# A hybrid decoder step on Trainium2: weight additions by feature tile, squares and forms of the last pair one product later, an embedding scaled on ScalarE

## The chip, the cores and the metric

The kernel runs on one core of one Trainium2 chip. The metric is the device time of one execution in microseconds (us); the median of three runs of the kernel before is 1403.98 us (1400.8 to 1405.53). A core has five engines that each take their instructions in order: TensorE (PE in the profile, with its weight loads as PEld), VectorE (DVE), ScalarE (ACT), GpSimd (POOL) and SyncE (SP), which here only issues DMA transfers. An instruction of one engine that needs the result of another waits at the head of its queue, and all that is queued behind it waits too.

## The reference, cut to what matters

One layer of a decoder on 1024 new prompt positions and 8 single new tokens (1032 columns in all): a mixer, a squared-ReLU MLP, and a per-layer input embedding, each added to the residual.

```python
x = x + jnp.concatenate([o, sg.astype(x.dtype)], axis=-1) @ w_out
x = x + jnp.square(jax.nn.relu(rms_norm(x, g_ff) @ w_up)) @ w_down
x = x + (p @ w_ple) * jax.nn.sigmoid(rms_norm(x, g_ple) @ w_ple_gate)
```

Here `w_up` is 1024 x 4096 and `w_down` 4096 x 1024. The change lies in the product with `w_down` and in the preparation of `p` (`p_prompt`, 1024 x 256). All arithmetic is float32.

## The kernel before, in words

Float32 products are made of three matmuls each: a weight block is split into a rounded part `whi` (ScalarE, line 150) and its remainder `wlo` (VectorE, line 153), the other operand into `hi` and `lo`, and whi·hi, wlo·hi and whi·lo are added in PSUM (lines 1473 to 1475). Such a pair `whi`, `wlo` is called a form here; a ring holds four of them.

The down projection (`down`, some 340 us of the span, from 905 to 1244 us) splits its 4096 rows into four groups j, and does each group by seven products in place of eight (P1, P6, P7, P4, P2, P5, P3 in that order, a scheme of Strassen's kind). That makes 28 products, n = 0 to 27, in the list `seq`. Each product has four feature tiles p, each with its own form, two token halves t, and 12 matmuls for each: 96 matmuls. PSUM results go by VectorE into `u2`, `u3` and `acc` (lines 1480 and 1482).

What a product needs:

- Its moving operand. It was computed by the up projection and lies in DRAM (`f_d`). `load_raw` (line 1356) brings it in two halves into the single buffer `raw`, ScalarE casts each half (`hi`, line 1363), VectorE subtracts (`lo`, line 1364). `split_raw(n + 1)` and `load_raw(n + 2)` stand at the start of product n.
- Its forms, taken four ahead from the generator `down_forms`. P1, P4, P2 take blocks of the weight as loaded (`a11`, `a22`, `a12`). P6 takes s2 = A21 + A22 - A11, P5 takes s1 = A21 + A22; GpSimd makes both for each p (lines 1385 and 1386). P7 and P3 take a difference `sd` (GpSimd, line 1392), in a buffer of which there is one only: the difference for tile p + 1 is not begun before `whi` and `wlo` of tile p have been made.

Three other pieces run in this stage. (1) The up projection's last pair of tiles is left over: its Relu and Square (ScalarE, line 1225, four passes over `q`) and its forms, six GpSimd subtractions (lines 1229 to 1231) into `late`, which is the memory of the accumulator C22; `dforms_out` (lines 1236 and 1237) stores both to `f_d`, where the products of the fourth group read them, and only then `x1_old` (line 1401) may load the old residual into C22. They stand in product n = 1, the stores in n = 2, the load in n = 3. (2) `x1_old` loads a quarter of the residual (1,056,768 bytes) into C11 at the start, C21 and C12 at n = 0 and 1. (3) `p_prompt` is loaded at the end of n = 12 into the memory of `q` (line 1526) and is scaled by the factor `mst` of its row: eight GpSimd multiplications of 128x256 (line 1530), written after n = 14 to 17.

The order on PE and SP is the one written in the program. On ScalarE, VectorE and GpSimd a scheduler chooses the order when the kernel is built, among instructions that are ready by its own estimate; `tc.high_priority` raises one, and `tc.issue_after(x)` keeps an instruction behind x.

## Time and profile before

| | |
|---|---|
| Median of the runs (lowest, highest) | 1403.98 us (1400.8, 1405.53) |
| The profiled execution's own time | 1404.94 us |
| Its span, first to last instruction | 1403.2 us |
| Mean granted clock of TensorE | 0.971 |
| Busy share of the span: PE, DVE, POOL, ACT | 94%, 64%, 51%, 46% |

The profile is of one execution. Times inside it count from the span's start; 1.74 us of the execution lie outside the span. A granted clock of 1.00 is TensorE's full speed (2.4 GHz), 0.50 its lower level. TensorE is busy for 94% of the whole; what it is not busy for, and where it runs at the lower level, has to be read from the single stretches.

### The profile page before, as it was taken

The numbers are of one execution on the slowest core, as the hardware profiler recorded it, in microseconds if no ns is written. First come the engines' busy times: TensorE is split into PE (matmuls) and PEld (weight loads), VectorE is DVE, ScalarE is ACT, GpSimd is POOL, SyncE is SP. The second block draws the span as 40 slices with busy tenths as digits, with TensorE's granted clock in tenths as the row PEclk, the third lists the DMA queues.
The fourth block names the chain that finished last, engine by engine and source line by source line (L and its number), as shares of the span: only waits on it lengthen the run. The fifth ranks groups of instructions, "written<-read, shape, count | busy, mean of one in ns | idle before, by whom it ended". The sixth has DMA issues, their size and how long they took to land.

```text
span 1403.2 us, 26599 instructions
## 1 busy us (share of the span) xinstructions
PE 1312.5 (94%) x10189; PEld 1280.5 (91%) x10189; DVE 900.7 (64%) x1836; ACT 645.6 (46%) x1353; POOL 708.8 (51%) x724
## 2 busy tenths in 40 slices
PE   6979978999999799899999999889998999899996
PEld 5879978888999799899999999889998999899996
DVE  7755745456946856555545544567976878797554
ACT  7574645632232415556545445443332333346344
POOL 5300888847515404668856787350516215835241
PEclk9999988999999999999999999999999999999998
DMA  7334534646524831244455564658353533232231
GB/s 237 101 91 107 153 92 137 177 135 174 150 84 146 259 90 46 61 137 130 150 149 169 175 212 155 221 191 283 117 184 113 172 122 121 61 102 78 63 121 61
DMA packets 213419, 194.00 MB, mean 138 GB/s; under 512 B 20952, under 2 KB 183451, under 8 KB 213284
## 3 DMA queue, kind: packets, MB, share of 16 engines
q1 hardware_dynamic: 213292, 192.30, 44.5%
q8 instruction: 80, 1.31, 0.4%
q14 instruction: 47, 0.39, 0.1%
HBM read 131.75 MB, written 60.61 MB: 137 GB/s over the span
## 4 chain that ended last, share of the span: by engine, by line
PE 69%; DVE 9%; POOL 9%; ACT 5%; issue 4%; DMA 3%; SPq 1%; POOLq 0%; ACTq 0%; DVEq 0%
PE A L1184 10%; PE D L1184 7%; PE d L1474 6%; PE d L1475 6%; PE d L1473 6%; PE g L209 5%; PE g L211 5%; PE g L210 5%; PE B L1184 3%; PE C L1184 3%; POOL xinv L644 2%; PE g L1702 2%; POOL it L643 2%; DVE wlo L153 2%; PE g L1704 2%
## 5 line engine op out<-in xcount | busy, mean ns | idle before, releaser
L209 PE MATMUL g<-ra,whi 128*128 128x384 f32 (+3 forms) x800 | 272.6, 341 | 0.7 <-ACT ra L388 0.6
L1474 PE MATMUL d<-h,wlo 128*128 128x260 f32 (+1 forms) x896 | 258.2, 288 | 11.0 <-DVE wlo L153 10.5
L1473 PE MATMUL d<-h,whi 128*128 128x260 f32 (+1 forms) x896 | 257.4, 287 | 7.9 <-ACT whi L150 7.9
L1475 PE MATMUL d<-h,whi 128*128 128x260 f32 (+1 forms) x896 | 257.3, 287 | 0.0
L211 PE MATMUL g<-ra,whi 128*128 128x384 f32 (+3 forms) x800 | 256.4, 321 | 0.8 <-POOL ra L389 0.4
L210 PE MATMUL g<-ra,wlo 128*128 128x384 f32 (+3 forms) x800 | 255.2, 319 | 0.0
L1474 PEld LDWEIGHTS d<-h,wlo 128*128 128x128 f32 x896 | 173.4, 194 | 13.3 <-DVE wlo L153 13.2
L1473 PEld LDWEIGHTS d<-h,whi 128*128 128x128 f32 x896 | 173.3, 193 | 8.9 <-ACT whi L150 8.9
L1475 PEld LDWEIGHTS d<-h,whi 128*128 128x128 f32 x896 | 173.2, 193 | 0.0
L209 PEld LDWEIGHTS g<-ra,whi 128*128 128x128 f32 x800 | 154.3, 193 | 2.9 <-ACT ra L388 1.0
L211 PEld LDWEIGHTS g<-ra,whi 128*128 128x128 f32 x800 | 153.7, 192 | 2.5 <-POOL ra L389 1.6
L210 PEld LDWEIGHTS g<-ra,wlo 128*128 128x128 f32 x800 | 154.7, 193 | 0.7 <-DVE wlo L153 0.3
L153 DVE TENSOR_TENSOR wlo<-s,whi 128x512 fp32r<-128x512 f32 x96 | 73.7, 769 | 80.8 <-ACT whi L150 80.4
L153 DVE TENSOR_TENSOR wlo<-st,whi 128x512 fp32r<-128x512 f32 x94 | 75.2, 801 | 39.9 <-ACT whi L150 39.1
L1184 PE MATMUL A<-fb,whi 128*128 128x260 f32 (+1 forms) x512 | 96.6, 281 | 0.0
L643 POOL TENSOR_TENSOR it<-ainv,xinv 32x31 f32<-32x31 f32 (+15 forms) x124 | 73.6, 594 | 39.6 <-DMA ainv<-inv_d 30.3
L150 ACT CAST whi<-s 128x512 fp32r<-128x512 f32 x96 | 59.3, 618 | 73.4 <-PE D L1184 29.1
L1363 ACT CAST h<-raw 128x1024 fp32r<-128x1024 f32 (+1 forms) x56 | 58.8, 1056 | 67.1 <-DMA raw<-f_d 34.7
L644 POOL TENSOR_TENSOR xinv<-xinv,it 32x31 f32<-32x31 f32 (+15 forms) x124 | 82.3, 664 | 9.6
L1225 ACT ACTIVATE q<-q 128x512 f32<-128x512 f32 (+2 forms) x124 | 77.5, 645 | 19.5 <-DVE q L1207 16.0
L1482 DVE TENSOR_TENSOR acc<-acc,d 128x256 f32<-128x256 f32 x192 | 75.0, 413 | 17.8 <-PE d L1475 16.8
L150 ACT CAST whi<-st 128x512 fp32r<-128x512 f32 x96 | 59.0, 619 | 58.2 <-PE g L211 31.4
(450 smaller groups left out, 3526.0 us busy)
## 6 DMA issues: line engine op xcount, KB each, us to landing
a<-in_w_down SPq DMA_DIRECT2D x16, 1024.0 KB
raw<-f_d SPq DMA_DIRECT2D x28, 520.0 KB
raw<-f_d SPq DMA_DIRECT2D x28, 512.0 KB
st<-in_w_in SPq DMA_DIRECT2D x24, 512.0 KB
ck<-ck_d SPq DMA_DIRECT2D x32, 320.0 KB
ra<-in_w_up SPq DMA_DIRECT2D x32, 256.0 KB
rb<-in_w_up SPq DMA_DIRECT2D x32, 256.0 KB
st<-in_w_ple_gate SPq DMA_DIRECT2D x16, 512.0 KB
```

The lines of the kernel that those rows point to most:

```text
L150: S.copy(dst_hi, src)
L153: lo_eng.tensor_sub(dst_lo, src, f32(dst_hi))
L209: PE.matmul(ps[:, :w], lhsT=whi[k], rhs=xh, start=(k == 0), stop=False)
L210: PE.matmul(ps[:, :w], lhsT=wlo[k], rhs=xh, start=False, stop=False)
L211: PE.matmul(ps[:, :w], lhsT=whi[k], rhs=xl, start=False, stop=(k == nk - 1))
L643: G.tensor_mul(tv, a, x)
L644: G.tensor_sub(X[:, j + 1 :, :w], X[:, j + 1 :, :w], tv)
L1184: PE.matmul(ps, lhsT=a[:, k, :], rhs=x[:, c, k, :], start=(first and k == 0 and j == 0), stop=(k == 3 and j == 2), skip_group_check=True)
L1225: placed["act"] = S.activation(v, v, func).ins
L1473: PE.matmul(ps, lhsT=wh[:, k, :], rhs=xh[:, k, :], start=(k == 0), stop=False)
L1474: PE.matmul(ps, lhsT=wl[:, k, :], rhs=xh[:, k, :], start=False, stop=False)
L1475: PE.matmul(ps, lhsT=wh[:, k, :], rhs=xl[:, k, :], start=False, stop=(k == 3))
```

## The change

There are four edits, all in the down projection.

1. In the first group (j = 0), s1 and s2 are kept in order tile by tile: s1 of tile p may not be issued before s2 of tile p - 1.
2. The squares and forms of the up projection's last pair move from product n = 1 to n = 2, behind the cast of product 2's input and behind the last difference issued so far; their stores move from n = 2 to n = 3, just ahead of the load into C22.
3. `x1_old(C11, 0, 0)` goes to the head of `down()`, ahead of the loads of the first input and of A11, A21 and A22 on SP.
4. The scaling of `p_prompt` becomes a ScalarE activation (Copy with a scale for each row), two of them in each of four products, each behind the cast `placed["cast", n]`.

```diff
                         if name == "P6":
-                            G.tensor_add(s1[:, p], a_of("A21", p), a_of("A22", p))
+                            with tc.issue_after(placed["sum"]) if j == 0 and p else ExitStack():
+                                G.tensor_add(s1[:, p], a_of("A21", p), a_of("A22", p))
                             placed["sum"] = G.tensor_sub(s2[:, p], s1[:, p], a_of("A11", p)).ins
...
-                            G.tensor_sub(f, *((a_of("A21", p), a_of("A11", p)) if name == "P7" else (a_of("A12", p), s2[:, p])))
+                            placed["sd"] = G.tensor_sub(f, *((a_of("A21", p), a_of("A11", p)) if name == "P7" else (a_of("A12", p), s2[:, p]))).ins
...
     def down():
+        x1_old(C11, 0, 0)
         load_raw(0)
         load_a(0, "A11")
         load_a(0, "A21")
         load_a(0, "A22")
-        x1_old(C11, 0, 0)
...
-                if n == 1 and p < 2:
+                if n == 2 and p < 2:
                     _, t, q = last[p]
-                    with tc.issue_after(placed["cast", 1]):
+                    with tc.issue_after(placed["cast", 2]):
                         squared(q)
-                    with tc.issue_after(placed["sum"]):
+                    with tc.issue_after(placed["sd"]):
                         dforms_of(t, q, late[t])
...
-            elif n == 2:
+            elif n == 3:
                 for p, t, q in last:
                     dforms_out(p, t, q, late[t])
-            elif n == 3:
                 x1_old(C22, 1, 1)
...
                     x = pt[:, pcol(nn, n - 14), :]
-                    G.tensor_scalar_mul(x, x, mst[:, nn, n - 14 : n - 13])
+                    with tc.issue_after(placed["cast", n]):
+                        S.activation(x, x, AF.Copy, scale=mst[:, nn, n - 14 : n - 13])
```

What this does to the queues is seen at three places. GpSimd first, in the first two products; `sd_11295` is the first difference of P7 (product 2), `s1_11090` and `s2_11091` the sums of the first group, `acc_11038` written from `q8_6118` the forms of the up projection's last pair. Before:

```order
L1392 TENSOR_TENSOR sd_11295<-a21_11069,a11_11072 128x512
L1385 TENSOR_TENSOR s1_11090<-a21_11069,a22_11068 128x512 x4
L1386 TENSOR_TENSOR s2_11091<-s1_11090,a11_11072 128x512 x4
L1229 TENSOR_TENSOR acc_11038<-q8_6118 128x2x256
L1230 TENSOR_TENSOR acc_11038<-q8_6118,acc_11038 128x256
```

After:

```order
L1386 TENSOR_TENSOR s1_11090<-a21_11069,a22_11068 128x512
L1387 TENSOR_TENSOR s2_11091<-s1_11090,a11_11072 128x512
L1386 TENSOR_TENSOR s1_11090<-a21_11069,a22_11068 128x512
L1387 TENSOR_TENSOR s2_11091<-s1_11090,a11_11072 128x512
L1386 TENSOR_TENSOR s1_11090<-a21_11069,a22_11068 128x512
L1387 TENSOR_TENSOR s2_11091<-s1_11090,a11_11072 128x512
L1386 TENSOR_TENSOR s1_11090<-a21_11069,a22_11068 128x512
L1387 TENSOR_TENSOR s2_11091<-s1_11090,a11_11072 128x512
L1393 TENSOR_TENSOR sd_11329<-a21_11069,a11_11072 128x512
L1393 TENSOR_TENSOR sd_11363<-a21_11069,a11_11072 128x512
L1393 TENSOR_TENSOR sd_11397<-a21_11069,a11_11072 128x512
L1229 TENSOR_TENSOR acc_11038<-q8_6118 128x2x256
```

The sums alternate, so that the second tile of s2 is the fourth operation and no longer the sixth, and the first one the second and no longer the fifth; the last pair's forms stand behind the remaining three differences of product 2.

VectorE in the same stretch; `h11_11066` is the remainder `lo` of product 1's input, `wlo_11147` and the names after it the remainders of s2's forms for product 1, `d_...` the PSUM results of product 0. Before:

```order
L1364 TENSOR_TENSOR h11_11066<-raw_11073,h10_11065 128x1024
L1480 COPY u2_11053<-d_11222 128x256
L1482 TENSOR_TENSOR acc_11038<-acc_11038,d_11222 128x256
L1364 TENSOR_TENSOR h11_11066<-raw_11073,h10_11065 128x1040
L1480 COPY u2_11053<-d_11237 128x260
L1482 TENSOR_TENSOR acc_11038<-acc_11038,d_11237 128x260
L153 TENSOR_TENSOR wlo_11147<-s2_11091,whi_11146 128x512
L153 TENSOR_TENSOR wlo_11183<-s2_11091,whi_11182 128x512
L153 TENSOR_TENSOR wlo_11219<-s2_11091,whi_11218 128x512
```

After:

```order
L1364 TENSOR_TENSOR h11_11066<-raw_11073,h10_11065 128x1024
L1481 COPY u2_11053<-d_11165 128x260
L1483 TENSOR_TENSOR acc_11038<-acc_11038,d_11165 128x260
L153 TENSOR_TENSOR wlo_11147<-s2_11091,whi_11146 128x512
L1481 COPY u2_11053<-d_11186 128x256
L1483 TENSOR_TENSOR acc_11038<-acc_11038,d_11186 128x256
L1364 TENSOR_TENSOR h11_11066<-raw_11073,h10_11065 128x1040
L1481 COPY u2_11053<-d_11201 128x260
L1483 TENSOR_TENSOR acc_11038<-acc_11038,d_11201 128x260
L153 TENSOR_TENSOR wlo_11183<-s2_11091,whi_11182 128x512
L1481 COPY u2_11053<-d_11222 128x256
L1483 TENSOR_TENSOR acc_11038<-acc_11038,d_11222 128x256
```

The first `wlo` of product 1 stands between the two halves of its input now, and the second one right behind the second half and one PSUM result; before, three of them stood together behind both halves and all of product 0's results.

ScalarE from product 0 to product 1; `h00_11070` is `hi` of product 2's input, line 1225 the Relu and Square of the last pair. Before:

```order
L1363 CAST h10_11065<-raw_11073 128x1024
L1363 CAST h10_11065<-raw_11073 128x1040
L1225 ACTIVATE q8_6118<-q8_6118 128x1024
L1225 ACTIVATE q8_6118<-q8_6118 128x1040
L150 CAST whi_11146<-s2_11091 128x512
L150 CAST whi_11182<-s2_11091 128x512
L1225 ACTIVATE q8_6118<-q8_6118 128x1024
L150 CAST whi_11218<-s2_11091 128x512
L1225 ACTIVATE q8_6118<-q8_6118 128x1040
L150 CAST whi_11254<-s2_11091 128x512
```

After:

```order
L1363 CAST h10_11065<-raw_11073 128x1024
L150 CAST whi_11146<-s2_11091 128x512
L1363 CAST h10_11065<-raw_11073 128x1040
L150 CAST whi_11182<-s2_11091 128x512
L1363 CAST h00_11070<-raw_11073 128x1024
L150 CAST whi_11218<-s2_11091 128x512
L1363 CAST h00_11070<-raw_11073 128x1040
L1225 ACTIVATE q8_6118<-q8_6118 128x1024
L1225 ACTIVATE q8_6118<-q8_6118 128x1040
L150 CAST whi_11254<-s2_11091 128x512
```

The third form's `whi` stands behind the first half of product 2's input now, the fourth behind both halves and two passes of line 1225.

GpSimd in product 13 (P3 of the second group), where `sd_12882` and `sd_12918` are the differences for its second and third tile. Before:

```order
L1385 TENSOR_TENSOR s1_12996<-a21_11069,a22_11068 128x512 x4
L1392 TENSOR_TENSOR sd_12882<-a12_11067,s2_12012 128x512
L1530 TENSOR_SCALAR q8_6118<-q8_6118,mst_6753 128x256 x8
L1392 TENSOR_TENSOR sd_12918<-a12_11067,s2_12012 128x512
L1392 TENSOR_TENSOR sd_12954<-a12_11067,s2_12012 128x512
```

After, on ScalarE in that product (`h00_11070` is the input of product 14):

```order
L1363 CAST h00_11070<-raw_11073 128x1024
L150 CAST whi_12884<-sd_12882 128x512
L1363 CAST h00_11070<-raw_11073 128x1040
L1531 ACTIVATE q8_6118<-q8_6118,mst_6753 128x256 x2
L150 CAST whi_12920<-sd_12918 128x512
L150 CAST whi_12956<-sd_12954 128x512
```

The eight multiplications are gone from between the two differences on GpSimd; two stand on ScalarE between the cast of product 14's second half and the `whi` of the third tile, and the other six follow in products 14 to 16.

## Rows read from the trace of the kernel before

**Rows 1.** Stretches: us; PE, PEld, DVE, ACT, POOL busy (count); PEclk; DMA share; GB/s.
```profile
910.00:924.10 14.10, 14.07 (x96) 13.89 (x96) 8.50 (x17) 7.52 (x10) 12.64 (x10) 0.81 0.42 155
924.10:928.90 4.80, 0.02 (x1) 0.00 (x0) 4.80 (x7) 1.65 (x2) 4.72 (x5) 1.00 0.51 141
928.90:932.40 3.50, 3.48 (x16) 3.48 (x17) 2.43 (x4) 1.06 (x1) 0.56 (x1) 0.51 0.98 345
932.40:1075.60 143.20, 142.49 (x1185) 141.49 (x1184) 112.44 (x195) 51.84 (x70) 42.29 (x30) 1.00 0.56 185
1079.10:1085.90 6.80, 5.50 (x24) 5.21 (x25) 3.61 (x4) 2.28 (x4) 5.27 (x5) 0.50 0.36 109
1198.60:1212.30 13.70, 9.47 (x48) 8.86 (x48) 7.60 (x8) 3.84 (x6) 13.70 (x10) 0.75 0.10 36
```

**Rows 2.** TensorE's timeline: start, duration, instruction [idle before, releaser], at four waits.
```profile
910.02 0.58 PE L1474 MATMUL d<-h,wlo 128*128 128x256 f32 x1 [3.62 <-DVE wlo L153]
...
928.92 0.58 PE L1474 MATMUL d<-h,wlo 128*128 128x256 f32 x1 [4.80 <-DVE wlo L153]
...
994.77 0.39 PE L1474 MATMUL d<-h,wlo 128*128 128x256 f32 x1 [0.34 <-DVE wlo L153]
...
1080.25 0.58 PE L1473 MATMUL d<-h,whi 128*128 128x256 f32 x1 [4.66 <-ACT whi L150]
```

**Rows 3.** VectorE's timeline, entry and first two products.
```profile
905.93 2.37 DVE L1364 TENSOR_TENSOR h<-raw,h 128x1024 fp32r<-128x1024 f32 x2
...
918.28 0.43 DVE L1480 COPY u<-d 128x260 f32<-128x260 f32 x1 [0.36 <-PE d L1475]
918.63 0.75 DVE L1482 TENSOR_TENSOR acc<-acc,d 128x260 f32<-128x260 f32 x2
...
921.84 2.26 DVE L1364 TENSOR_TENSOR h<-raw,h 128x1024 fp32r<-128x1024 f32 x1
...
924.68 2.35 DVE L1364 TENSOR_TENSOR h<-raw,h 128x1040 fp32r<-128x1040 f32 x1
...
927.62 2.99 DVE L153 TENSOR_TENSOR wlo<-s,whi 128x512 fp32r<-128x512 f32 x3
```

**Rows 4.** GpSimd's timeline, first two products.
```profile
911.34 5.29 POOL L1385 TENSOR_TENSOR s<-a,a 128x512 f32<-128x512 f32 x4 [1.92 <-DVE wlo L153]
916.59 5.07 POOL L1386 TENSOR_TENSOR s<-s,a 128x512 f32<-128x512 f32 x4
```

**Rows 5.** ScalarE's timeline, entry and first two products.
```profile
902.63 1.06 ACT L1363 CAST h<-raw 128x1040 fp32r<-128x1040 f32 x1 [0.29 <-DMA raw<-f_d]
905.35 2.18 ACT L150 CAST whi<-a 128x512 fp32r<-128x512 f32 x4 [1.66 <-DMA a<-in_w_down]
...
917.62 2.01 ACT L1225 ACTIVATE q<-q 128x1024 f32<-128x1024 f32 x2
919.54 1.12 ACT L150 CAST whi<-s 128x512 fp32r<-128x512 f32 x2
...
927.38 1.05 ACT L1363 CAST h<-raw 128x1024 fp32r<-128x1024 f32 x1 [2.67 <-DMA raw<-f_d]
```

**Rows 6.** The stretch of the loads at the stage's entry, columns as in Rows 1.
```profile
895.10:905.30 10.20, 10.20 (x89) 10.20 (x87) 4.20 (x10) 2.86 (x4) 0.00 (x0) 1.00 1.02 349
```

**Rows 7.** Chain of waits back from product 13: start, duration, what.
```profile
1061.02 8.03 DMA q<-in_p_prompt
...
1069.14 9.18 POOL q L1530 x8
```

**Rows 8.** Timelines of ScalarE and VectorE in product 13, one line each.
```profile
1069.84 1.06 ACT L1363 CAST h<-raw 128x1040 fp32r<-128x1040 f32 x1
...
1071.28 0.68 DVE L153 TENSOR_TENSOR wlo<-sd,whi 128x512 fp32r<-128x512 f32 x1
1071.88 1.23 DVE L1364 TENSOR_TENSOR h<-raw,h 128x1040 fp32r<-128x1040 f32 x1
```

**Rows 9.** ScalarE in this stage by line and shape: count | busy us, mean ns.
```profile
L166 ACT ACTIVATE xs<-acc,vec 128x516 fp32r<-128x516 f32 x8 | 5.7, 717 | 2.0 <-DVE acc L1482 1.9
```

## The prediction

> **What bounds the kernel now.** TensorE is busy for 94% of the span, so I read first the stretches in which it is not, then, for each, what ended its wait, and last what the releasing engine had been doing. Most of the down projection gives nothing away: in the 143 us from 932.4 to 1075.6 TensorE is busy for 142.5 at full clock [rows 1]. The pace of a product follows from its first stretch: 96 matmuls in 14.1 us at a mean granted clock of 0.81 are 14.1 x 0.81 = 11.4 us at full clock, so 2.85 us for a tile (24 matmuls) and 0.12 us for a matmul [rows 1].
>
> Two waits of TensorE over 4 us stand inside this stage, and after each the clock is at its lower level (1.2 GHz) for a while.
>
> Wait A, 4.80 us before 928.92, ended by a `wlo` on VectorE [rows 2]. The weight sums are not what is late there: GpSimd ended s2 at 921.7 [rows 4], and the first two `whi` were cast by 920.7 [rows 5]. VectorE had the two halves of the next input ahead of the `wlo` in its queue: 2.26 us from 921.84 and 2.35 us from 924.68, and only from 927.62 the `wlo` [rows 3]. In the 4.8 us VectorE is busy all the time, and GpSimd for 4.72 of them [rows 1]. Such a half takes 1.23 us where GpSimd stands still [rows 8]. So the order on VectorE and GpSimd's work beside it made this wait. After it, 16 matmuls take 3.50 us at clock 0.51 [rows 1], 3.5 - 16 x 0.12 = 1.6 us too long.
>
> Wait B, 4.66 us before 1080.25, ended by a `whi` on ScalarE [rows 2]. The chain behind it: the load of `p_prompt`, 8.03 us from 1061.02, then eight scalings on GpSimd, 9.18 us from 1069.14, and only then the difference `sd` that this `whi` is cast from [rows 7]. After it, 24 matmuls fill the 5.65 us from 1080.25 to 1085.9 at clock 0.50 [rows 1, 2], 5.65 - 2.85 = 2.8 us too long.
>
> A short wait is different: 0.34 us at 994.77 [rows 2] lies within the long stretch whose mean clock is 1.00 [rows 1]; it costs its own length. A third slow place, 13.7 us from 1198.6 for 48 matmuls [rows 1], lies in the last group, which none of the edits reaches; it stays.
>
> **Scaling on ScalarE (edit 4): takes wait B away.** With the eight scalings gone from GpSimd's queue, `sd` for the third tile follows as soon as its one buffer is free, which is when the second tile's `wlo` ends, 1071.28 + 0.68 = 1071.96 [rows 8]. A difference takes about 1.3, as one of the sums [rows 4], `whi` 0.6 [rows 5], `wlo` 0.68 [rows 8]: 1071.96 + 1.3 + 0.6 + 0.7 = 1074.6, against 1080.25 - 4.66 = 1075.6 at which TensorE wants it [rows 2]; margin 1.0 us. The fourth tile follows 2.6 us later and is wanted 2.85 us later, so it holds too. Between the cast of product 14's second half, which ends at 1070.9 [rows 8], and the `whi` of the third tile, ScalarE now does two scalings. No row has a scaling of 128x256 on ScalarE: the nearest is a scaled activation of 128x516 at 0.717 us [rows 9], so 0.36 (in proportion) to 0.72 (as long) each; I take 0.5. They end at about 1071.9 (at the latest 1072.4), ahead of the 1073.3 at which `sd` is ready: nothing on the path. They wait for the load, which lands at 1061.02 + 8.03 = 1069.05 [rows 7], 1.85 us before they are reached. The other six stand in products 14 to 16, some 0.5 us each beside an engine that is mostly idle. Saved: 4.66 + 2.8 = 7.5 us.
>
> **Sums by tile, and squares and forms one product later (edits 1 and 2): take wait A away, if nothing else in product 1 is late.** GpSimd's eight sums took 5.29 + 5.07 us, the first s2 being the fifth [rows 4]; in turns it is the second. The sums start at about 913.3, since A22 lands some 2 us later (below), so the first s2 is there at 913.3 + 2.6 = 915.9, where it was 916.59 + 1.3 = 917.9; the last ends at 923.7. VectorE's new order (front part, the change) starts with the first half at about 917.6. It runs beside GpSimd, so 2.3 us [rows 3], to 919.9; a PSUM result (1.1 us for its pair of operations [rows 3]); the first `wlo` at 1.0 [rows 3]: done near 921.5. Then a result to 922.2, the second half at 1.7 (GpSimd's sums end in the middle of it, and GpSimd then waits for the single buffer of `sd`), a result, and the second `wlo` at 0.7: done near 925.4. The third stands behind the first half of product 2's input. Its load may start when VectorE has read the raw half (919.9) and lands 3.28 us later (924.10 to 927.38 in the trace [rows 3, 5]), at 923.2; cast 1.05, subtraction 1.23, a result, `wlo`: 928.6. The fourth `whi` stands on ScalarE behind both casts of that input and two passes over `q`, 2.01 us [rows 5]: 931.0 to 931.6, so the fourth `wlo` at 931.7 to 932.3. TensorE wants the four at 924.1 (928.92 - 4.80 [rows 2]) and then every 2.85, so 927.0, 929.8 and 932.6: margins 2.6, 1.6, 1.2 and 0.3 to 0.9. In product 2 each tile needs, in a single buffer, `sd` 1.3, `whi` 0.6 and `wlo` 0.7 [rows 4, 5, 8] with queueing about 2.85, which is TensorE's pace; there I count on small waits. I take two of the size of 0.34 [rows 2], 0.7 us in all, as what is left; the bounds are 0 and 4.7 (a wait of 3 us, two thirds of A, and 1.7 of slow clock after it).
>
> The squares and forms themselves, six operations on GpSimd of about 1.3 each [rows 4] and four passes on ScalarE, now stand in product 2 behind all its differences and end at about 950. Their stores wait on SP for the last of them; behind them stand C22's load, and the load of product 6's input, which can't start before product 5's input has left the raw buffer, at about 960. 1.85 MB of stores and 1.06 MB of load at 349 GB/s [rows 6] are 8.3 us beside TensorE's work, to about 959, and C22 is first added to in the sixth product, from 924.1 + 4 x 11.4 = 970 on. So no cost; were the forms 10 us later than I think, both would begin to be late.
>
> Saved by edits 1 and 2: 4.80 + 1.6 - 0.7 = 5.7 us.
>
> **The residual's load first (edit 3): near nothing.** It puts 1.06 MB ahead of the first input and of A11 on DMA engines that are full at that point (busy share 1.02, 349 GB/s [rows 6]): 1.06 MB / 349 GB/s = 3.0 us. The second half of the first input, cast from 902.63 [rows 5], comes to about 905.6; VectorE reached the input only at 905.93 [rows 3], being on the up projection's last results until then, so this half is not felt. A11's first cast goes from 905.35 [rows 5] to 908.4, and the first `wlo` is then ready at 908.4 + 0.6 + 0.7 = 909.7, against 910.02 in the trace [rows 2], where VectorE was slowed by the two halves before it. So TensorE starts as before: -0.3 to 0; if the load holds up the transfers by twice its own time, +3.0. I take 0. A22 comes some 2 us later (its own load was behind A21 and can't start before TensorE leaves its memory).
>
> On VectorE beside GpSimd the rows show more than a factor's worth of spread: a half is 2.26 to 2.35 with GpSimd at work and 1.23 without [rows 3, 8], so a delay of about 1.1, a little less than one GpSimd sum of 1.3 [rows 4]; rival 1 carries this through. The Trainium skill (SBUF — State Buffer, section "SBUF: two separate sides") says that a VectorE operation with two SBUF inputs and a GpSimd operation take a shared port pair as an exclusive lock for a whole instruction, and that the other one is fully blocked. By that rule a half or a `wlo` beside GpSimd could come up to a whole GpSimd operation of 1.3 late, and rival 1 would be 0.4 later for its two delays.
>
> **The sum**, against the profiled execution: 1404.94 - 7.5 - 5.7 - 0 = 1391.7 us. That execution is 0.96 above the median of the runs (1403.98), so against the median 1390.8, and rounded 1390.5, since the entry's bound reaches 0.3 below nothing.
>
> **Rivals.**
> 1. *The wait of product 1 moves to a later tile.* GpSimd's differences for product 2 fall beside VectorE's second half and the third and fourth `wlo`, each 1.1 late [rows 3, 8]: the fourth, with a margin of 0.3 to 0.9 and two such delays ahead of it, comes 1.3 to 1.9 late, and the same in one tile of product 2. A wait of that size may bring the lower clock for a tile, 1.6 [rows 1]. For it: VectorE's doubled durations; against: GpSimd mostly stands still there for want of the buffer. 1390.5 + 1.6 + 1.6 = about 1393.5, up to 1395.
> 2. *The entry starts later.* The load first costs TensorE its own 3.0 us or a part of it, since A11 is what TensorE begins with: 1391.5 to 1393.5. Against: VectorE's `wlo` and not A11 ended the wait there [rows 2].
> 3. *The change does not do what it says for one wait:* the scheduler's order holds, but `whi` of the third tile in product 13, or VectorE in product 1, is held as long as before. Then only 5.7 or 7.5 of the 13.2 come: 1398 or 1396.
> 4. *Slower: ScalarE's queue waits for `p_prompt`.* On GpSimd the load held only differences; on ScalarE it holds every cast of the stage behind it. It decides when the load lands more than 1.85 us (its lead) + 1.0 (the margin) = about 2.8 us later than in the trace; beyond that TensorE loses one for one. To end slower than before by 4.2 us it must land some 13.2 + 4.2 + 2.8 = 20 us later, in 28 us and not 8.03 [rows 7]. Against: 8.03 us for its 1.05 MB is already long beside 349 GB/s [rows 6], and no row shows a cause for another 20.
>
> **How the numbers follow.** Forecast 0.70 (1388.5 to 1392.5), rival 1 0.17, rival 2 0.07, rival 3 0.03, rival 4 0.03. Range 1387 to 1396: down by the spread of the runs before (3.2 below their median) and no residue, up to the end of rival 1; rivals 3 and 4 are mostly outside. A measurement of this kernel tells 0.3% (4.2 us) from no change. The forecast and rivals 1 and 2 are all faster by more than that, as is rival 3: faster 0.94; within 0.3%: 0.03, where rival 4 is half way or two rivals add up; slower 0.03.
>
> **What would show it.** In the profile after: no wait of TensorE over 1 us between 911 and 1195; `wlo` of s2 one by one between the halves on VectorE, the first before 922; the differences of product 13 in a row with no gap on GpSimd, and two scalings on ScalarE of 0.36 to 0.72 us each beside them; a mean granted clock of about 0.973. Wrong would be: a wait for `wlo` or `whi` over 1 us at the third or fourth tile of product 1 or in product 2 (rival 1), the first `wlo` of the stage after 910.5 (rival 2), scalings that begin late and wait for a DMA (rival 4).

## The result, and the profile after

The changed kernel takes 1395.35 us (median of 13 runs, 1391.49 to 1404.17), the kernel before 1404.64 us (13 runs, 1400.8 to 1407.8): 9.3 us less, a ratio of 0.994 (95% interval 0.9925 to 0.9954). Forecast were 1390.5 us, 13.2 us less (0.991 of the profiled execution). The direction is right, the size is not: 1404.64 x 0.994 is 1396.2, just above the end of the range (1396), and the interval goes from 1394.1 to 1398.2. The median alone lies just inside that end, 4.9 us above the forecast.

The profiled execution of the changed kernel took 1393.05 us, its span 1391.3. Line 1 of its page:

```profile
PE 1306.6 (94%) x10189; PEld 1275.8 (92%) x10189; DVE 901.3 (65%) x1836; ACT 648.6 (47%) x1361; POOL 703.0 (51%) x716
```

TensorE's waits of over 0.3 us between the end of the up projection and product 23, from its timeline (columns as in [rows 2]):

```profile
907.76 0.56 PE L1474 MATMUL d<-h,whi 128*128 128x256 f32 x1 [3.09 <-ACT whi L150]
...
982.84 0.38 PE L1474 MATMUL d<-h,whi 128*128 128x256 f32 x1 [0.90 <-ACT whi L150]
983.56 0.39 PE L1475 MATMUL d<-h,wlo 128*128 128x256 f32 x1 [0.34 <-DVE wlo L153]
...
988.78 0.39 PE L1475 MATMUL d<-h,wlo 128*128 128x256 f32 x1 [2.06 <-DVE wlo L153]
```

Both waits of [rows 2] that the change was aimed at are gone: none is left in product 1, none over 0.3 us in product 13. In their place stand three in product 6 (P3 of the first group), where the kernel before had two of 0.23 and 0.34 us. Products 1, 6 and 13 of the changed kernel as stretches (columns as in [rows 1]):

```profile
921.20:932.80 11.60, 11.60 (x99) 11.50 (x98) 10.28 (x18) 7.62 (x10) 7.78 (x5) 1.00 0.94 327
978.90:996.00 17.10, 13.80 (x98) 13.18 (x97) 14.77 (x25) 5.43 (x8) 11.65 (x9) 0.90 0.32 109
1064.80:1076.90 12.10, 11.92 (x98) 11.53 (x97) 10.09 (x15) 4.89 (x9) 8.26 (x6) 1.00 0.30 101
```

The same three products of the kernel before:

```profile
923.80:941.80 18.00, 13.20 (x98) 12.99 (x97) 13.92 (x22) 5.02 (x6) 8.16 (x7) 0.91 0.82 270
987.70:1000.90 13.20, 12.49 (x98) 11.71 (x97) 10.99 (x15) 4.48 (x7) 9.23 (x7) 1.00 0.27 93
1069.70:1088.90 19.20, 14.40 (x99) 13.89 (x98) 11.53 (x16) 4.10 (x7) 17.67 (x15) 0.82 0.29 100
```

Product 1 gives 6.4 us and product 13 gives 7.1; product 6 takes 3.9 back, 1.7 of it by a clock of 0.90 in place of 1.00 (17.1 x 0.10).

All kernels below are compared by such stretches, from the start of one product's first matmul to that of the next in TensorE's timeline. "Entry" is from the end of the up projection's last matmul to the start of product 0's second tile, "stage" from that end to the end of the last matmul of product 27. Times in us, one trace for each row:

| trace | up projection ends | entry | product 1 | 6 | 13 | 23 | stage |
|---|---|---|---|---|---|---|---|
| before | 905.6 | 9.59 | 17.99 | 13.26 | 19.16 | 19.77 | 354.5 |
| after, first trace | 904.7 | 7.88 | 11.57 | 17.14 | 12.11 | 20.51 | 343.8 |
| after, second | 907.4 | 8.50 | 11.40 | 15.53 | 12.12 | 19.78 | 341.9 |
| after, third | 903.4 | 10.15 | 11.40 | 16.13 | 12.12 | 19.74 | 344.2 |
| b1, scaling only | 912.3 | 9.59 | 17.75 | 12.67 | 12.12 | 20.51 | 347.5 |
| b2, sums in turns only | 908.6 | 9.58 | 15.22 | 11.53 | 18.14 | 18.25 | 349.0 |
| b3, forms later only | 908.6 | 9.58 | 13.15 | 17.21 | 19.68 | 19.65 | 354.1 |
| b4, residual's load last | 909.4 | 9.58 | 12.11 | 14.11 | 12.12 | 19.42 | 343.7 |
| a1, stores early | 905.2 | 7.74 | 11.47 | 14.88 | 12.12 | 19.78 | 340.9 |
| a4, C22 behind input | 909.2 | 7.77 | 11.70 | 12.14 | 12.12 | 19.73 | 338.4 |
| c1, sums behind differences | 912.3 | 10.33 | 11.40 | 11.53 | 11.40 | 19.47 | 338.3 |
| d1, a4 and c1 | 908.6 | 7.54 | 11.50 | 11.53 | 11.40 | 20.47 | 336.9 |
| d2, residual's load second | 907.6 | 8.52 | 14.69 | 11.53 | 11.40 | 19.45 | 340.6 |
| d3, additions behind too | 907.7 | 7.58 | 11.79 | 11.53 | 11.40 | 11.40 | 335.5 |

A product without a wait takes 11.4 to 11.5 us. By the stage the change saves 10.7, 12.5 and 10.2 us in its three traces.

Each ratio below is to the kernel before as it was timed beside that kernel. Its median was 1405.77 us beside a1, a2, a4 and b1, 1404.65 beside b2, b3, b4 and c1, and 1403.42 beside a5, d1, d2 and d3, so medians of different groups do not compare as they stand.

### The profile page after: what moved, and what is told of

It is laid out like the page before. It is cut to its first block, busy times and chain, and to the rows that moved or that the text cites. A ratio compares the mean times of both kernels' runs of the same rounds, so it can differ in the third digit from the quotient of the medians.

```text
span 1391.3 us, 26609 instructions
## 1 busy us (share of the span) xinstructions
PE 1306.6 (94%) x10189; PEld 1275.8 (92%) x10189; DVE 901.3 (65%) x1836; ACT 648.6 (47%) x1361; POOL 703.0 (51%) x716
## 4 chain that ended last, share of the span: by engine, by line
PE 69%; POOL 11%; DVE 8%; issue 4%; ACT 4%; DMA 3%; SPq 1%; POOLq 0%; ACTq 0%; DVEq 0%
PE A L1184 9%; PE d L1475 7%; PE d L1476 6%; PE d L1474 6%; PE D L1184 6%; PE g L209 5%; PE g L211 5%; PE g L210 5%; PE C L1184 3%; POOL xinv L644 3%; PE B L1184 3%; POOL it L643 3%; PE g L1703 2%; PE g L1705 2%; PE g L1704 2%
## 5 line engine op out<-in xcount | busy, mean ns | idle before, releaser
L1474 PEld LDWEIGHTS d<-h,whi 128*128 128x128 f32 x896 | 171.6, 191 | 9.1 <-ACT whi L150 9.1
L1476 PEld LDWEIGHTS d<-h,whi 128*128 128x128 f32 x896 | 171.1, 191 | 0.0
```

The source lines that it names most:

```text
L1474: PE.matmul(ps, lhsT=wh[:, k, :], rhs=xh[:, k, :], start=(k == 0), stop=False)
L1476: PE.matmul(ps, lhsT=wh[:, k, :], rhs=xl[:, k, :], start=False, stop=(k == 3))
```

## What holds product 6

The chain of waits of the changed kernel, back from product 6 (start, duration, what):

```profile
965.04 6.29 DMA raw<-f_d
971.41 1.06 ACT h L1363
972.49 0.58 DVE h L1364
973.19 0.45 issue
973.64 0.70 DVE wlo L153
974.40 6.47 POOL s L1386 x4
980.87 1.27 POOL sd L1393
```

`raw<-f_d` at 965.04 is the load of product 6's input. SP's queue says why it is issued no earlier:

```profile
951.07 2.40 SPq L1356 DMA_DIRECT2D raw<-f_d  x2
953.53 0.43 SPq L1236 DMA_DIRECT2D f_d<-q  x1
954.05 0.44 SPq L1237 DMA_DIRECT2D f_d<-acc  x1
954.54 0.93 SPq L1236 DMA_DIRECT2D f_d<-q  x1
955.52 1.29 SPq L1237 DMA_DIRECT2D f_d<-acc  x1
964.03 0.91 SPq L1402 DMA_DIRECT2D acc<-x_d  x2
965.04 1.11 SPq L1356 DMA_DIRECT2D raw<-f_d  x2
```

The four stores of the last pair go out at 953.5, behind the two halves of product 5's input. C22's load overwrites what they read and is held on SP until 964.0, and the input behind it too. The DMA engines in that time (columns as in [rows 1]):

```profile
953.50:956.00 2.50, 2.50 (x24) 2.50 (x23) 2.48 (x6) 1.48 (x2) 0.00 (x0) 1.00 0.84 199
956.00:962.00 6.00, 6.00 (x53) 6.00 (x52) 4.75 (x9) 2.28 (x4) 0.00 (x0) 1.00 1.03 333
962.00:964.00 2.00, 2.00 (x19) 2.00 (x18) 1.47 (x3) 0.55 (x1) 0.00 (x0) 1.00 0.05 16
```

These are 2.53 MB: the 1.85 MB of the stores and the rest of product 5's input, for whose second half ScalarE waits until 957.25. So the stores, issued from 953.5 on, run behind that input on the engines, near the rate of the loads at the stage's entry (349 GB/s [rows 6]). SP then waits 7.2 us for the last of them, the final 2 us at 16 GB/s. VectorE, which takes that input in order, stands still for 4.38 us until 972.49; behind it in its queue is the last remainder of s1 (973.64); the next group's four s1 on GpSimd reuse the memory that this remainder reads; and behind those four stands the second difference of product 6. So there are three links: the transfers, VectorE's order, and GpSimd's order. The runs below cut the first and the third, one at a time and together; no run cuts the second. In the kernel before, the stores stood ahead of product 5's input, at 948.79 where TensorE was 8.8 us later.

## The experiments

**a1: the stores back at the end of product 2** (rest as changed).

```diff
-            elif n == 3:
+            elif n == 2:
                 for p, t, q in last:
                     dforms_out(p, t, q, late[t])
+            elif n == 3:
                 x1_old(C22, 1, 1)
```

> The changed kernel with one step put back: the stores of the last pair's squares and forms stand on SP at the end of product 2 again, ahead of the input load for product 5, and no longer at the end of product 3. Theory (late transfers): in the changed kernel the stores run from 953.5 to 964, C22's load waits for them on SP, product 6's input load stands behind that, and VectorE waits 4.38 us for this input; the 3.9 us that TensorE loses in product 6 come from there. Put back, the loss goes: TensorE starts tile 1 of product 7 some 8.8 us ahead of the kernel before, not 4.9, and the time is 1395.4 - 3.9 = 1391.5 us, a ratio to before of 0.991. Rival (GpSimd's order): the four sums s1 of the next group stand ahead of the second difference of product 6 and hold it, whatever the transfers do; then TensorE still waits 2 to 3 us in product 6 and the time stays at 1395.

Measured 1392.78 us (6 runs), ratio to before 0.992 (0.990 to 0.994); product 6 takes 14.88 us, between the two expectations: 2.3 less than in the first trace, 0.65 less than in the second, and 1.6 more than before the change. SP shows that the input's load is not earlier:

```profile
951.70 2.42 SPq L1356 DMA_DIRECT2D raw<-f_d  x2
958.05 1.96 SPq L1402 DMA_DIRECT2D acc<-x_d  x2
964.80 1.82 SPq L1356 DMA_DIRECT2D raw<-f_d  x2
```

C22's load leaves 6 us earlier, but product 6's input only 0.2: the raw buffer comes free late, because product 5's input, which now stands behind the stores, needs 10.75 us from its issue to its landing (3.5 at most in the changed kernel, where its cast begins at 954.60), and ScalarE's cast waits for it until 962.47. From the chain of waits:

```profile
951.70 10.75 DMA raw<-f_d
...
964.80 3.51 DMA raw<-f_d
```

Product 6's input, with C22's load out of its way, lands after 3.51 us where the changed kernel needed 6.29, so VectorE waits 1.01 us for it and not 4.38. The edit hands a part of the delay from one input to another: the input comes some 3 us earlier, and the loss shrinks to 1.6 us. That fits the theory, but the edit does not cut the first link.

**a4: C22's load behind product 6's input.**

```diff
                     dforms_out(p, t, q, late[t])
+            elif n == 4:
                 x1_old(C22, 1, 1)
```

> The changed kernel with the load into C22 one product later on SP, behind the input load for product 6; the stores stay at the end of product 3. Theory (the input is what is late): product 6's input no longer waits for the stores to end, so VectorE does not stand still for it before 973, and the loss in product 6 shrinks from 3.9 to under 1 us: 1392 us. Rival (the accumulator C22 is what is late): its load now lands later still, VectorE's additions of product 5 wait for it, and the loss stays or grows: 1395 to 1398 us.

Measured 1391.59 us (4 runs), ratio 0.9905 (0.988 to 0.993); product 6:

```profile
983.40:995.50 12.10, 11.95 (x98) 11.61 (x97) 10.08 (x15) 4.07 (x7) 8.27 (x6) 1.00 0.31 100
```

The loss is gone, though C22 itself comes later (its load is issued at 969.48, on a clock some 4.5 us later than in the changed kernel). The late input is the first link; C22's lateness costs nothing that shows here.

**c1: the next group's s1 behind the last difference, on GpSimd.**

```diff
-                            with tc.issue_after(placed["sum"]) if j == 0 and p else ExitStack():
+                            with tc.issue_after(placed["sum" if j == 0 else "sd"]) if j or p else ExitStack():
```

> The changed kernel, with the sums s1 of groups 1 to 3 kept behind the last difference of the group before on GpSimd; stores and loads stay where they are. Theory (the late input is the first link, and reaches TensorE through the four sums that wait on VectorE and stand ahead of the second difference of product 6): VectorE still stands still for the input of product 6 before 973, but the second difference starts by about 978.5 on the changed kernel's clock, and the loss in product 6 falls from 2.3 to 3.9 us to 1 us or less: 1392 us. Rival (the late input alone sets it, by VectorE's backlog): the loss in product 6 stays over 2 us, 1395 us. In both a wait of under 1 us may come up in the second product of a group, whose sums are now made later.

Measured 1391.13 us (4 runs), ratio 0.990 (0.988 to 0.992). VectorE still waits for product 6's input, 2.74 us, and product 6 loses nothing:

```profile
980.61 1.23 DVE L1364 TENSOR_TENSOR h<-raw,h 128x1024 fp32r<-128x1024 f32 x1 [2.74 <-ACT h L1363]
```
```profile
988.60:1000.10 11.50, 11.50 (x98) 11.50 (x97) 10.64 (x18) 3.88 (x6) 9.06 (x6) 1.00 0.41 133
```

GpSimd begins the second difference at 985.60, 3.0 us ahead of product 6, where it began 1.9 us behind its start in the changed kernel; the input itself is 1.6 us earlier on that clock. So the late input reaches TensorE through GpSimd's order. The rival is refuted, and product 13, whose differences stand behind such sums as well, goes to 11.40. No wait came up in the second products of the groups.

**d1: the edits of a4 and c1 together.**

> The changed kernel with two more edits: the load into C22 behind the input load for product 6 on SP, and the sums s1 of groups 1 to 3 behind the last difference of the group before. Theory (both cut the same chain, at its first and at its third link): no more is gained than by one of them; product 6 takes 11.5 us (17.1 and 15.5 in the two traces of the changed kernel), the down projection 16 to 16.5 us less than in the kernel before, the time 1391 us. Rival (they are two separate losses, of which each removes one): the stage gains 18 us or more, the time is 1389 us or less.

Measured 1389.15 us (5 runs), ratio 0.989 (0.9875 to 0.991). Product 6 takes the 11.53 us of c1: two cuts of one chain, as the theory has it. The time is all but the rival's (1389 or less), and the stage gains 17.6 us, between the two. But the kernel before was faster beside d1 too: against it d1 saves 14.3 us, a4 14.2 and c1 13.5, and the three intervals overlap, so the times do not tell the three kernels apart. Nor does the stage's difference come from product 6: against c1 the trace gains 2.8 us at the entry and loses 1.0 in product 23, against a4 it gains 0.7 in product 13 and 0.6 in product 6.

**b1: edit 4 alone on the kernel before.**

```diff
-                    G.tensor_scalar_mul(x, x, mst[:, nn, n - 14 : n - 13])
+                    with tc.issue_after(placed["cast", n]):
+                        S.activation(x, x, AF.Copy, scale=mst[:, nn, n - 14 : n - 13])
```

> The kernel before with edit 4 alone, the embedding scaled on ScalarE. Theory (the waits are separate): wait B in product 13 goes with the slow clock behind it, 7.1 us as in the changed kernel, and wait A stays: 1404.6 - 7.1 = 1397.5 us, ratio 0.995. Rival (ScalarE takes up what GpSimd gives back): the differences come on time but the casts behind the scalings are late, and more than 1 us of the wait stays: 1399 to 1404 us.

Measured 1398.38 us (10 runs), ratio 0.995 (0.993 to 0.997); product 13 takes 12.12 us as in the changed kernel, 7.0 less than before, and wait A stays (product 1 takes 17.75). The changed kernel's ScalarE there:

```profile
1064.91 1.06 ACT L1363 CAST h<-raw 128x1040 fp32r<-128x1040 f32 x1
1065.88 0.91 ACT L1531 ACTIVATE q<-q,mst 128x256 f32<-128x256 f32 x2
1069.37 0.62 ACT L150 CAST whi<-sd 128x512 fp32r<-128x512 f32 x1 [2.59 <-POOL sd L1393]
```

The two scalings take 0.91 us, 0.5 each as estimated, wait for nothing, and leave 2.59 us before the cast.

**b2 and b3: edits 1 and 2 apart, on the kernel before.** b2:

```diff
-                            G.tensor_add(s1[:, p], a_of("A21", p), a_of("A22", p))
+                            with tc.issue_after(placed["sum"]) if j == 0 and p else ExitStack():
+                                G.tensor_add(s1[:, p], a_of("A21", p), a_of("A22", p))
```

> The kernel before with edit 1 alone, the sums s1 and s2 of the first group in turns. VectorE's queue then has the first wlo of product 1 ahead of both halves of its input, the second between them, and the last pair's forms stay on GpSimd beside them. Theory (VectorE's order made wait A): the 4.80 us go, at most 1 us of waits is left in product 1, which takes under 13 us from its first matmul to product 2's, where the kernel before takes 18.0. Rival (GpSimd's six forms beside VectorE made it): at least 2 us of wait remain in product 1, at its second to fourth tile.

b3, with the stores moved as in the change:

```diff
-                if n == 1 and p < 2:
+                if n == 2 and p < 2:
...
-            elif n == 2:
+            elif n == 3:
                 for p, t, q in last:
                     dforms_out(p, t, q, late[t])
-            elif n == 3:
                 x1_old(C22, 1, 1)
```

> The kernel before with edit 2 alone, the last pair's squares, forms and stores one product later; the sums are four s1, then four s2. The first wlo of product 1 stands behind both halves on VectorE as before, but the halves no longer run beside the six forms. Theory (VectorE's order made wait A, GpSimd's work beside it only lengthened it): halves of 1.23 us, the first wlo at about 925.8 on the clock of the kernel before, so a wait of 1.7 us stays in product 1. Rival (GpSimd's forms beside it made all of it): under 0.5 us stays. In both, product 6 loses 2 to 4 us against the kernel before, since the stores stand where they stand in the changed kernel.

b2: 1400.88 us (6 runs), ratio 0.997 (0.995 to 0.999). b3: 1406.46 us (8 runs), ratio 1.0005 (0.999 to 1.002). TensorE's wait in product 1, of b2 and then of b3:

```profile
930.70 0.39 PE L1476 MATMUL d<-h,whi 128*128 128x260 f32 x1 [2.00 <-DVE h L1364]
```
```profile
928.65 0.39 PE L1474 MATMUL d<-h,wlo 128*128 128x256 f32 x1 [1.49 <-DVE wlo L153]
```

b3 does what its theory says, 1.49 us against 1.7 expected: without the forms beside them the halves take 1.30 and 1.23 us, but the `wlo` still stands behind both. b2 does what neither says: the `wlo` is on time, and now the second half itself (`h`) is late, 2.00 us, with a lower clock of 0.69 in the 3.4 us behind it. VectorE has one queue, and each edit alone lets the other thing in it be late. Product 1 gains 2.8 us by b2, 4.8 by b3 and 6.4 to 6.6 by both. b3 also shows the price of edit 2 alone: it gains 4.8 us in product 1, loses 4.0 in product 6 (17.21), and as a whole is no faster.

**b4: the changed kernel without edit 3.**

```diff
-        x1_old(C11, 0, 0)
         load_raw(0)
         load_a(0, "A11")
         load_a(0, "A21")
         load_a(0, "A22")
+        x1_old(C11, 0, 0)
```

> The changed kernel without edit 3: the residual's load into C11 behind A22 again. By the traces with edit 3 the stretch from the up projection's last matmul to the second tile takes 7.7 to 8.5 us, without it 9.6 us. Theory (edit 3 itself gave the 1.1 to 1.8 us, since it keeps GpSimd's first difference, and with it the lock on VectorE's first wlo, away from that wlo by bringing A21 later): 9.6 us again, and the wlo takes 1.7 us again; the time is 1395.3 + 1.5 = 1396.8 us. Rival (as predicted, the load is neutral, and the shorter entry has another cause): 8.5 us or less, 1395 us.

Measured 1396.99 us (4 runs), ratio 0.992 (0.990 to 0.995). The entry takes 9.58 us, as in all five traces with this load behind A22. The first row is b4's VectorE there, the second the changed kernel's:

```profile
912.04 2.95 DVE L153 TENSOR_TENSOR wlo<-a,whi 128x512 fp32r<-128x512 f32 x3
```
```profile
907.74 1.90 DVE L153 TENSOR_TENSOR wlo<-a,whi 128x512 fp32r<-128x512 f32 x3 [0.32 <-ACT whi L150]
```

The first three remainders take 2.95 us where GpSimd's first difference falls beside them (911.79 to 913.25 in b4) and 1.90 where it comes later. That much of the theory holds. But the gain is not certain: with the load first the entry took 7.54 to 7.88 us in five traces, and 8.50, 10.15 and 10.33 in three, where A11, behind the load, lands later: its first cast begins 3.1 to 3.8 us after the up projection's end there, 1.9 to 2.4 in the five (in the third trace of the changed kernel ScalarE waits 3.38 us for it):

```profile
907.13 2.18 ACT L150 CAST whi<-a 128x512 fp32r<-128x512 f32 x4 [3.38 <-DMA a<-in_w_down]
```

The whole time does not show a gain by edit 3: b4's ratio of 0.992 is no worse than the changed kernel's 0.993 to 0.994, and its stage (343.7 us) is within the changed kernel's (341.9 to 344.2). Its product 6, 14.11 us, loses less than in the other four traces with edit 2 and no cure, and 0.95 us of wait stand in its product 2.

**d2: the load behind A11 and ahead of A21** (rest as d1).

```diff
     def down():
-        x1_old(C11, 0, 0)
         load_raw(0)
         load_a(0, "A11")
+        x1_old(C11, 0, 0)
         load_a(0, "A21")
```

> As d1, with the residual's load into C11 behind the first input and A11, still ahead of A21 and A22. Theory (the load's place ahead of A21 is what keeps GpSimd's first difference, and with it the slow wlo, off VectorE; its place ahead of A11 only costs, 4.5 us of wait in one trace of five): the stretch from the up projection's last matmul to the second tile takes 8.5 us or less in every trace, where it was 7.7 to 10.3 us with the load first and 9.6 us with it last; the time is that of d1 or 0.5 us less. Rival (A11's lateness is what helps, since TensorE then starts once and not twice): 9.3 us or more, the time is 1 us more than that of d1.

Measured 1391.53 us (5 runs), ratio 0.991 (0.990 to 0.993), 2.4 us more than d1. The entry, 8.52 us, is what the theory says and not the rival's 9.3, but product 1 takes 14.69 us: the scheduler has put VectorE's first half of product 1's input behind six results, so that it starts at 923.18, and the first `wlo` behind it is late by 1.45 us. The idea isn't refuted, and this build of it is no better.

**d3: the last group's additions on GpSimd behind the differences** (rest as d1).

```diff
                     def add(x, y):
-                        G.tensor_add(x[:, p], x[:, p], y[:, p])
+                        with tc.issue_after(placed["sd"]):
+                            G.tensor_add(x[:, p], x[:, p], y[:, p])
```

> As d1, with GpSimd's additions of the last group (into U3, C12, C21, C22) each kept behind the last difference issued. In the kernel before and the changed one, TensorE waits 4.2 to 5.6 us in product 23 for forms whose differences stand behind such additions, and runs at the lower clock after it, 7 to 9 us in all. Theory (GpSimd's order makes this loss): it goes but for 2 us, and the time is 1391 - 5 = 1386 us. Rival (TensorE or VectorE is what these additions wait for, and the later ones are missed elsewhere): the loss moves to the products after it, and the time stays at 1391.

Measured 1386.02 us (4 runs), ratio 0.987 (0.985 to 0.989): the fastest of all, 8.5 us under the changed kernel timed beside it (a5). Product 23 falls from 20.47 to 11.40 us. In the profiled execution, though, most of it comes back in product 25, which takes 18.86 us and not 11.40:

```profile
1213.93 0.58 PE L1475 MATMUL d<-h,wlo 128*128 128x256 f32 x1 [4.86 <-DVE wlo L153]
```

There VectorE is late: its remainders take up to 1.46 us beside GpSimd's additions, which now stand in two rows of six (from 1184.15 and from 1197.21), and its halves 2.31 and 1.98 beside the sums of squares that follow them (`ss`, line 1413). The stage gains 1.4 us against d1's trace, the median 3.1. Both theory and rival hold in part.

**a2 and a5: the changed kernel twice more.**

> The changed kernel once more, on the same chip as the others of this call. Theory (the spread of its runs, 1391 to 1404 us, is the clock and the waits of the stages outside the down projection): its down projection reads as in the first trace to within 0.5 us at every product, the loss in product 6 included, and what differs between the two traces lies before 905 us or after 1250 us; median near 1395. Rival (the margins within the down projection are so thin that waits come and go there): the places where TensorE gains or loses against the kernel before differ by more than 1 us inside the stage.

> The changed kernel a third time, beside the three variants on one chip. Theory: product 6 takes 15 to 17.5 us again and the entry 7.7 to 10.4 us, median 1395 us, so 4 us above d1 and 9 us above d3. Rival (the loss in product 6 comes and goes with what the stages before leave): a trace in which product 6 takes under 13 us, and a median within 1.5 us of that of d1.

Medians 1395.12 (6 runs) and 1394.52 us (6 runs), ratios 0.993 both. The loss in product 6 stands in all three traces, 2.3 to 3.9 us, so it is no accident of one run; its size, and the entry, vary by more than the 0.5 us that I expected. Product 6 takes 14.1 to 17.2 us in the five traces with edit 2 and no cure for it (b3 and b4 among them), 11.5 to 13.3 in the three without edit 2. The part ahead of the stage, which no edit touches, differs too: the up projection ends between 903.4 and 907.4 us in the three traces, and between 903.4 and 912.3 in all of the table.

## Why the prediction was right or wrong

**Wait B (7.5 us saved): right.** 7.0 us in every trace, by b1 through edit 4 alone. Product 13 stays 0.7 us above 11.4, small waits that go in c1, so they come from GpSimd's sums ahead of the differences.

**Wait A (6.4 saved, less 0.7): right, and the residue was not needed.** Product 1 saves 6.4 to 6.6 us. VectorE's times in the changed kernel, 2.6 us ahead of the kernel before there, are near the working: the four `wlo` end at 918.8, 922.7, 926.7 and 929.9; TensorE begins the tiles at 921.2, 924.1, 926.9 and 929.8. The margins fall from tile to tile, as forecast, to nothing at the last. The halves beside GpSimd's sums took 1.55 to 1.66 us, which lies between the 2.3 and the 1.23 that I had rows for. Rival 1, the wait moved to a later tile, did not come in the changed kernel; d2's wait of 1.45 us stands at the first tile.

**The stores and loads of edit 2 (nothing): wrong, and this is the step that failed.** It said that stores and load together take 8.3 us at 349 GB/s from about 950, and end at 959, before product 6's input can be loaded at 960. The forms were ready in time (948.7), the raw buffer was free in time (959.6), and the rate was near (333 GB/s from 956 to 962). What was wrong is the order: the stores stood on SP behind the second half of product 5's input and went out at 953.5, shared the DMA engines with it, and the load could not run with them, since it waits for their end, 964.0. So the input's issue came at 965.0 and not at 960, and with C22's load on the engines ahead of it it landed only at 971.3, after 6.29 us (3.51 in a1). I priced a row of transfers by bytes and left out that one waits for the other on a queue that holds a third. I also named the point from which it costs, "10 us later", where 5 were enough, because I looked at what C22 and the input are due for and not at who else stands behind VectorE's wait: the last remainder of s1, the next group's four sums, and behind them the difference for product 6. Cost: 2.3 to 3.9 us, and my sign "no wait over 1 us between 911 and 1195" failed there (2.06 us at 988.78). None of the four rivals had it: the median is close to rival 1's number (1393.5, up to 1395), but not by its mechanism.

**The entry (nothing, 0.3 faster to 3.0 slower): half right.** The load costs A11 its place as estimated (first cast 2.6 us later against the end of the up projection, 3.0 forecast). What I missed is the share of the lock, by which VectorE and GpSimd hold each other up (below): the later A21 takes GpSimd's difference away from the first `wlo`. d2, which has the quick remainders but A11 at its old place, shows it alone: an entry of 8.52 us, 1.1 less than before. The rest seems to come, though no run tried it by itself, where A11's lateness turns TensorE's start and stop into about one start: product 0 of the first trace runs at a mean clock of 0.87, where it was 0.81 [rows 1]. That is not certain either: in the third trace, with one start after a wait of 4.4 us, it is 0.81 again. Over three traces: 1.7 and 1.1 us saved, 0.6 lost.

**The sum.** 6.5 + 7.0 + 0.7 (entry, mean of three) - 3.0 (product 6, mean of three) = 11.2, the mean by the stage (10.7, 12.5, 10.2), where 13.2 were forecast; without the loss in product 6 it would have been about 14. The medians of the runs gave 8.9 to 10.7 in three comparisons; the spread ahead of the stage does not let them be told from 11.2, so it stays open whether the runs really gain less than the stage. One slip in the chances: rival 3 is faster by its own times, so that "faster" adds up to 0.97 and not 0.94.

**The lock** (the Trainium skill, SBUF — State Buffer, section "SBUF: two separate sides": whichever of the two engines starts first has the port pair for its whole instruction) shows where a single operation is met: 2.95 us for three remainders and not 1.90, 1.05 more, under one GpSimd operation of 1.46. It also sets the length of the halves. In the changed kernel, GpSimd's sum, VectorE's half that begins during it, and GpSimd's next sum:

```profile
918.32 1.62 POOL L1387 TENSOR_TENSOR s<-s,a 128x512 f32<-128x512 f32 x1
```
```profile
919.38 1.66 DVE L1364 TENSOR_TENSOR h<-raw,h 128x1040 fp32r<-128x1040 f32 x1
```
```profile
919.90 2.29 POOL L1386 TENSOR_TENSOR s<-a,a 128x512 f32<-128x512 f32 x1
```

When the half begins, the running sum has 0.56 us left, and the half takes 0.56 + 1.10; the next sum begins under the half and takes 2.29 where 1.28 is its length alone. So it is in this stage of all 14 traces: a half that begins more than 0.1 us before the end of a GpSimd sum, addition or difference takes what is left of that and 1.08 to 1.11 us more, and one that begins beside none of them takes 1.21 to 1.24. The traces agree with the page: a half waits for one whole operation at most, and mostly for the rest of one. My reading of [rows 8], that GpSimd stands still beside the half of 1.23 us, was wrong: its eight scalings ran from 1069.14 to 1078.32 [rows 7], and why they did not lengthen that half no run shows. The figure itself is right.

## What to carry to other kernels

When a store moves on an in-order DMA queue, write down what stands behind it that waits for its end, and follow that to the end of its chain: a load that overwrites what the store reads holds everything behind it, and bytes over a rate do not price that. A store moved ahead of a load makes that load late instead (a1). An edit that is free for its own results can still reorder the queue of an engine whose scheduler sees other ready times (d2): read the order of the built kernel again after each. And compare by stretches of the trace: here the traces spread by 9 us ahead of the stage that was changed, as much as the whole gain.

## What was not expected of the hardware

- A wait of 1.49 us in product 1 left the clock at 1.00 in the 3.4 us after it, one of 2.00 us was followed by 0.69:

```profile
928.60:932.00 3.40, 3.35 (x28) 3.35 (x29) 3.40 (x7) 1.05 (x1) 0.00 (x0) 1.00 0.85 236
```
```profile
930.70:934.10 3.40, 3.40 (x20) 3.40 (x21) 3.40 (x6) 1.70 (x3) 3.40 (x4) 0.69 0.68 190
```

The length of the wait does not settle it: product 6 of the changed kernel has the same wait, 2.06 or 2.07 us, in its three traces, and the clock behind it is 0.64, 1.00 and 0.53. Much of product 6's spread is this.

```profile
988.80:992.20 3.40, 3.40 (x19) 3.40 (x20) 2.34 (x5) 1.66 (x3) 3.31 (x3) 0.64 0.29 59
```
```profile
991.10:994.50 3.40, 3.22 (x25) 3.01 (x25) 2.33 (x5) 1.96 (x4) 3.26 (x3) 1.00 0.20 30
```
```profile
988.30:991.70 3.40, 3.37 (x16) 3.37 (x17) 2.35 (x5) 1.66 (x3) 3.27 (x3) 0.53 0.27 34
```

- The same VectorE subtraction of 128x1024 takes 1.21 to 2.35 us, and what sets it is how much of a GpSimd sum or difference is left when it begins (the lock, above).
- The four stores of 1.85 MB to DRAM are not slower than loads: the DMA engines move 333 GB/s from 956 to 962 while most of them run, against 349 in a stretch of loads [rows 6]. What is long is the way around it, 10.5 us from the first store's issue to that of the load that waits for the last.
